# A list-scheduled DeltaNet stage: planner costs from a trace, query decays subtracted on VectorE, first values loaded on their own, output-norm Newton steps on GpSimd

## The chip, the cores and the metric

The kernel runs on one core of a Trainium2 chip. Time is device time in microseconds (us) of one execution. The engines are named as the profile names them: PE is TensorE's matmul row (PEld its weight loads), DVE is VectorE, ACT is ScalarE, POOL is GpSimd, SP is SyncE, whose queue issues most of the DMAs. A row that ends in "q" (SPq, ACTq) is an engine's instruction queue: semaphore waits and DMA issues.

## What is computed

Two layers over 512 latent tokens and 256 context tokens of width 1024, batch 1. Each layer is adaLN-modulated RMSNorm, a mixer, a SiLU gate and a gated residual. Layer 0, which the change is about, is a bidirectional gated DeltaNet with 8 query/key heads and 16 value heads of 128, in chunks of 64 tokens:

```python
p   = u @ w_in                                   # 1024 x 6208
qkv = silu(centred_dwconv(p[..., :4096], conv_w))    # 5 taps; z = the next 2048 columns
beta = sigmoid(ab[:, :, 0]);  g = -exp(a_log) * softplus(ab[:, :, 1] + dt_bias)
gc    = cumsum(g) within a chunk
decay = exp(where(lower, gc[:, None] - gc[None, :], -inf))
a     = where(strict, (k*beta) @ k.T * decay, 0)
t_inv = inverse of (eye + a)                     # unit lower triangular, 64 x 64
qk    = q @ k.T * decay
v_new = t_inv @ (v*beta) - (t_inv @ (k*beta*exp(gc))) @ S
o     = (q*exp(gc)) @ S + qk @ v_new;   S = S*exp(gc_last) + k_dec.T @ v_new
y     = (rms_norm(o) * silu(z)) @ w_out
```

Both directions are run; the state S left by the context is the start for the latents. Layer 1 is grouped-query attention with rotary positions, and the change leaves its code as it is.

## The kernel before

**Stages.** Layer 0 runs in two stages. In the first, up to about 552 us of the profiled execution, everything but the recurrence is made: the adaLN products, the in-projection, the decays, the inverses and q k^T, most of it stored to DRAM buffers (`k_d`, `q_d`, `z_d`, `v_d`, `t_d`, `qk_d`, `gc_d`). In the second, from about 552 to 735 us, the recurrence reads these back, two value heads at a time and 48 steps `x`; the out-projection and layer 1 follow.

**Tiles.** Tokens stand in 6 tiles of 128 (2 of context, 4 of latents). Names carry the tile, `0m` to `5m` for the key side ("m": the matrices to be inverted) and `0q` to `5q` for the query side, and a variant `v` of 0 or 1 for the direction. A decay tile `df` is 128 partitions x 16 heads x 64 columns. f32 products are made of three passes with high and low parts: a weight tile `w` is loaded, ACT writes its high part `wh`, and DVE or POOL writes the rest, `wl = w - wh` (L874).

**The in-projection.** After 8 key heads come 40 heads in the order of a string, "z" and "q" and "v" (L858), each of 24 matmuls of 512 and 24 of 256 columns (`gemm_part`, L885), in one of four PSUM buffers "g". A head's buffers come free when ACT and DVE have run its taps (`acc`, L892 and L900) and its SiLU (`sil_z` L917, `sil_v` L919), so late work on DVE stops PE two or three products later.

**The inverses.** For each tile `t`: a key gram on PE (`G`, L723), masked by DVE and ACT; the decays; products `md`, `mo` of decay and gram on DVE (L672); a transposition on DVE (`L`, L753) and a product with beta on POOL (L758). Two tiles make a pair, and POOL solves three pairs (`X0`, `X1`, `X2`) one after the other: a clearing, then 31 columns of two instructions each (L771, L772), then a weighing with beta (L776; that of `X2` on DVE). Then for each tile the joins: two transpositions `U` on DVE (L790), products `pp` (L799) and `pw` (L823) on PE, and `Tt` on ACT (L811, L830), stored to `t_d`. The query side has its own grams (`GQ`, L840), masks on DVE (`KQ`, L849), decays, and a product on POOL (L672) that is stored to `qk_d` (L855).

**The decays, before.** The rows of `gc` are loaded into `df`, spread over the partitions (`decay_rows`, L686). For m tiles 0 and 1 POOL subtracts a column from all heads in one instruction (`apart`, L705) and ACT makes Abs and Exp of it (`faded`, L710, L711). For the ten other tiles ACT does it alone: one Abs with a bias for each of 16 heads (L698) and one Exp (L700), for both variants.

**What sets the order.** The first stage is written out by a list planner (`written_out`, L1039). Each piece of work has an engine, a cost, a due time, what it comes after, and what buffers it takes and holds (`pool_of`, L1005). The planner gives the next place to the piece that can start first by its own sums (`ready_at`, with a margin for each engine), the one with the lower due time among equals. Costs and due times are thus only numbers in the planner: they set the order of instructions on every engine, and nothing else. Semaphores hold the chip to the dependences, and an instruction that waits holds all that is behind it on its engine.

**Around the recurrence.** The loads for its first step are pieces of the first stage: `first_matrices` (T, QK and the keys) and, after that, `first_values` in two halves (`v_d0`, `v_d1`, L972). DMAs that SP and ACT issue share eight completion semaphores in turn, so that an issue waits for the landing of the DMA eight before it. In steps `x` of 43 to 46 a list `chain` is worked off: the factors of the output norm, for which DVE runs three Newton steps of an inverse root (`rsqrt_steps`, L200 to L202) on 128 x 48 numbers, 3, 3, 3 and then all that is left.

## Time and profile before

| | us |
|---|---|
| time, three runs | 1178.34, 1169.69, 1173.31 (median 1173.31) |
| the profiled execution: its time | 1172.76 |
| its span, first to last instruction | 1171.0 |
| PE busy in it | 1127.3 (96%) |
| DVE, ACT, POOL busy | 784.0, 734.9, 602.6 |
| first stage, PE's first instruction of the recurrence | at 552.01 |
| POOL's solves, first clearing to the end of X2 | 236.19 to about 470.8 |
| mean granted clock of TensorE | 0.989 |

The profile shows one execution. A row of the chain, the waits or the timeline names engine, line, operation and tile; what stands in brackets is idle time of the engine just ahead of that row and what ended it. The granted clock is the share of full clock that TensorE was given.

### The profile page before, as it was taken

To read this page: it belongs to the slowest core of one execution; us is meant where nothing else is said; L and a number is where in the kernel's file an instruction comes from. 1 tells how busy PE (TensorE), PEld (TensorE's weight loads), DVE (VectorE), ACT (ScalarE), POOL (GpSimd) and SP (SyncE) were. 2 spreads that over 40 slices of the span, in tenths; PEclk is the share of its full clock that TensorE was granted. 3 is DMA by queue.
4 is the path that set the end of the run, shared out by engine and by line. 5 is a ranking of instruction groups with operands and counts; after the bars stand their busy time and mean duration, and the time that the engine had idled before them with its cause. 6 is when DMAs were issued, how large, how long until landed. Compare 5 with 4: busy or idle time off the path is not lost. (4 is left out here: it accounts for less than half of the span.)

```text
span 1171.0 us, 27730 instructions
## 1 busy us (share of the span) xinstructions
PE 1127.3 (96%) x10767; PEld 923.8 (79%) x10767; DVE 784.0 (67%) x1645; ACT 734.9 (63%) x1938; POOL 602.6 (51%) x478
## 2 busy tenths in 40 slices
PE   6999999999999799998999999999999999999996
PEld 4777788888888688887666666788887889999885
DVE  5686464899886686873778888345557476667646
ACT  5435544668795966594678998775753246666731
POOL 0252020399999999740475585555744153130810
PEclk9999999999999999999999999899999999999999
DMA  9767745666654834778999993585844112101323
GB/s 366 265 267 265 262 127 176 181 194 177 171 185 153 276 114 150 243 248 248 266 249 251 281 260 96 191 220 183 248 135 135 37 55 73 37 19 55 108 72 90
DMA packets 118901, 208.73 MB, mean 178 GB/s; under 512 B 12497, under 2 KB 77170, under 8 KB 114930
## 3 DMA queue, kind: packets, MB, share of 16 engines
q1 hardware_dynamic: 98834, 195.32, 54.6%
q10 hardware_dynamic: 19936, 11.64, 3.4%
q8 instruction: 85, 1.39, 0.5%
q14 instruction: 46, 0.38, 0.1%
HBM read 166.16 MB, written 40.67 MB: 177 GB/s over the span
## 5 line engine op out<-in xcount | busy, mean ns | idle before, releaser
L1624 PE MATMUL po<-woh,y 128*128 128x512 f32 x384 | 130.3, 404 | 0.3 <-ACT y L1600 0.3
L1466 POOL TENSOR_TENSOR S<-S,glb 128x512 f32<-128x512 f32 x80 | 81.7, 1042 | 75.5 <-PE ks L1457 75.5
L1573 POOL TENSOR_TENSOR wol<-wo,woh 128x1024 fp32r<-128x1024 f32 x32 | 77.1, 2412 | 55.9 <-ACT woh L1566 52.9
L772 POOL TENSOR_TENSOR X<-X,tmp 128x62 f32<-128x62 f32 (+15 forms) x93 | 98.0, 1053 | 7.3
L900 DVE SCALAR_TENSOR_TENSOR acc_v<-g_v,cwv,acc_v 128x510 f32<-128x510 f32 (+3 forms) x128 | 78.2, 614 | 25.1 <-ACT acc_v L892 21.7
L885 PE MATMUL g_z<-uh,wh_z 128*128 128x512 f32 (+1 forms) x256 | 88.0, 344 | 4.7 <-DVE sil_v L919 4.7
L771 POOL TENSOR_TENSOR tmp<-L,X 128x62 f32<-128x62 f32 (+15 forms) x93 | 86.6, 931 | 6.8
L885 PE MATMUL g_v<-uh,wh_v 128*128 128x512 f32 (+1 forms) x256 | 88.1, 344 | 0.0
L885 PE MATMUL g_v<-uh,wl_v 128*128 128x512 f32 (+1 forms) x256 | 86.6, 338 | 0.3 <-issue 0.3
L885 PE MATMUL g_v<-ul,wh_v 128*128 128x512 f32 (+1 forms) x256 | 86.6, 338 | 0.0
L885 PE MATMUL g_z<-uh,wl_z 128*128 128x512 f32 (+1 forms) x256 | 86.1, 336 | 0.0
L885 PE MATMUL g_z<-ul,wh_z 128*128 128x512 f32 (+1 forms) x256 | 86.1, 336 | 0.0
L1624 PEld LDWEIGHTS po<-woh,y 128*128 128x128 f32 x384 | 72.8, 190 | 15.7 <-ACT y L1600 0.7
L1624 PE MATMUL po<-wol,y 128*128 128x512 f32 x192 | 76.1, 396 | 0.3 <-POOL wol L1573 0.3
L1598 DVE SCALAR_TENSOR_TENSOR pt<-pt,og,z 128x128 f32<-128x128 f32 x96 | 34.4, 358 | 34.2 <-PE pt L1589 31.2
L885 PEld LDWEIGHTS g_z<-uh,wh_z 128*128 128x128 f32 x256 | 48.5, 190 | 10.0 <-DVE sil_v L919 5.1
L1531 DVE TENSOR_TENSOR S<-su,S 128x512 f32<-128x512 f32 x80 | 51.6, 687 | 6.0 <-PE su L1517 3.9
L1457 PE MATMUL ks<-S,ck 128*64 128x256 f32 x352 | 55.2, 392 | 0.4 <-ACT o L1463 0.4
L473 DVE SCALAR_TENSOR_TENSOR acc_k<-g_k,cwv,acc_k 128x510 f32<-128x510 f32 (+3 forms) x64 | 39.3, 615 | 22.7 <-ACT acc_k L466 21.0
L885 PEld LDWEIGHTS g_v<-uh,wh_v 128*128 128x128 f32 x256 | 49.2, 192 | 5.7 <-issue 0.4
L885 PEld LDWEIGHTS g_v<-uh,wl_v 128*128 128x128 f32 x256 | 49.1, 192 | 5.2
L885 PEld LDWEIGHTS g_v<-ul,wh_v 128*128 128x128 f32 x256 | 49.1, 192 | 4.8
(440 smaller groups left out, 3336.5 us busy)
## 6 DMA issues: line engine op xcount, KB each, us to landing
aw<-in_ada_late SPq DMA_DIRECT2D x16, 1024.0 KB, 8.5
wo<-in_dn_w_out SPq DMA_DIRECT2D x32, 512.0 KB, 3.9
cv<-v_d SPq DMA_DIRECT2D x48, 256.0 KB, 8.0
aw<-in_ada_first SPq DMA_DIRECT2D x8, 1024.0 KB, 12.3
w_z<-in_dn_w_in SPq DMA_DIRECT2D x16, 512.0 KB, 4.1
w_v<-in_dn_w_in SPq DMA_DIRECT2D x16, 512.0 KB, 4.0
v_d<-vt ACTq DMA_DIRECT2D x16, 384.0 KB, 4.2
cT<-t_d SPq DMA_DIRECT2D x12, 512.0 KB, 8.1
```

What stands on the lines that cost most here:

```text
L473: V.scalar_tensor_tensor(acc[:, c0 + lo:c0 + hi], ps[:, lo + j - 2:hi + j - 2], cwv[:, j, 8 + h:9 + h], acc[:, c0 + lo:c0 + hi], ALU.mult, ...
L771: G.tensor_tensor(tv, bcast(L[:, :, j + 1:, j], 3, j + 1), bcast(X[:, :, j, 0:j + 1], 2, n), ALU.mult)
L772: G.tensor_tensor(X[:, :, j + 1:, 0:j + 1], X[:, :, j + 1:, 0:j + 1], tv, ALU.subtract)
L885: T.matmul(ps[:, :m], w[:, k], u[:, k, c0:c0 + m], start=k == 0 and n_ == 0, stop=k == KT - 1 and n_ == 2)
L900: V.scalar_tensor_tensor(acc[:, c0 + lo:c0 + hi], ps[:, lo + j - 2:hi + j - 2], cwv[:, j, ct:ct + 1], acc[:, c0 + lo:c0 + hi], ALU.mult, A ...
L1457: T.matmul(ks[r0:r0 + 64, w], kq[w][:, hh, r0:r0 + 64], St[hh][:, d], start=True, stop=True)
L1466: G.tensor_tensor(St[hh], St[hh], bcast(g_, 3, P), ALU.mult)
L1531: V.tensor_tensor(St[hh], sj, St[hh], ALU.add)
L1573: G.tensor_tensor(wl, raws.pop(n), halves[n][0], ALU.subtract)
L1598: V.scalar_tensor_tensor(pj, pj, og, raw(z, off, [[st_, 2], [1, 64]]), ALU.mult, ALU.mult)
L1624: T.matmul(acc[:, nh], y[i][:, j, :], ww[k][:, nh * 512:(nh + 1) * 512], start=h == 0 and x == 0, stop=h == VH - 1 and x == 2)
```

## The change

It has four parts.

1. **The list.** Planner costs are replaced by other numbers for many pieces, the due times of grams, joins and query products are changed, the head order is another string, and `wl` of heads 4, 33 and 34 goes from POOL to DVE. The cost of a solve's column stays.
2. **Decays.** `apart` takes an engine from a table. m tiles 0 and 1 stay on POOL; m tiles 2 and 5 and q tiles 0, 1, 2, 4 and 5 are subtracted by DVE, q tile 3 by POOL, each in one instruction for a variant, and ACT then makes one Abs and one Exp of 128 x 1024. m tiles 3 and 4 keep the 16 Abs with bias.
3. **First values.** The first half of `first_values` no longer comes after `first_matrices`, and is due 20 us earlier than the matrices.
4. **Output norm.** For context and the first latents (`gi` 0) the Newton steps are 12 instructions of 128 x 48 on POOL behind two on DVE; the chain is worked off 4, 6, 6 and the rest.

```diff
+    def pool_steps(x, mul):
...
+        steps = [
+            lambda: V.tensor_scalar(x, x, mul, EPS, ALU.mult, ALU.add),
+            lambda: V.tensor_scalar(y.bitcast(I32), x.bitcast(I32), -0.5, float(0x5F3759DF), ALU.mult, ALU.add),
+        ]
+        for i in range(3):
+            to = x if i == 2 else y
+            steps += [
+                lambda: G.tensor_tensor(t, y, y, ALU.mult),
+                lambda: G.tensor_tensor(t, t, x, ALU.mult),
+                lambda: G.tensor_scalar(t, t, -0.5, 1.5, ALU.mult, ALU.add),
+                lambda to=to: G.tensor_tensor(to, t, y, ALU.mult),
+            ]
+        return steps
...
-    def apart(t, v, rows):
+    def apart(t, v, rows, E):
 
         df = dfs[t, v]
-        G.tensor_tensor(df, df, bcast(rows[:, v, t], 2, 64), ALU.subtract)
+        E.tensor_tensor(df, df, bcast(rows[:, v, t], 2, 64), ALU.subtract)
...
-    order = "zqzqzqqzqqzqzqvvzvvzvvzvvzvvzvvzvvvzvzzz"
+    order = "zqzqqqqzzqzqzqvvvzvzvvzvvzvvzvvzvvvzvzzz"
...
-        G_ = n in (1, 2, 3, 4, 33, 34, 35, 36, 37, 38, 39)
+        G_ = n in (1, 2, 3, 35, 36, 37, 38, 39)
...
-                tp_ = Piece("DVE", (3.3, 1.9)[i], e + (0.5, 2.4)[i], taps, n, i, after=[ce], holds=[("g", g[i]), ("acc", a_[0])], lands=0.1)
+                tp_ = Piece("DVE", (3.2, 1.75)[i], e + (0.5, 2.4)[i], taps, n, i, after=[ce], holds=[("g", g[i]), ("acc", a_[0])], lands=0.1)
...
+    APART = (("G", "G", "V", "", "", "V"), ("V", "V", "V", "G", "V", "V"))
+
     def decays(t, r, due, rows):
         out_ = []
         for v in range(2):
             d_ = [r[v]]
-            if t in ((0, 1) if rows is gcM else ()):
-                d_.append(Piece("POOL", 2.5, due + 3 * v - 3, apart, t, v, rows, after=d_, holds=[("df", r[v])], lands=0.1))
+            E = APART[rows is gcV][t]
+            if E:
+                d_.append(Piece({"G": "POOL", "V": "DVE"}[E], {"G": 2.2, "V": 1.25}[E], due + 3 * v - 3, apart, t, v, rows, G if E == "G" else V, after=d_, holds=[("df", r[v])], lands=0.1))
...
-    for t, due in enumerate(T0 + x for x in (26, 0, 100, 136, 140, 175)):
+    for t, due in enumerate(T0 + x for x in (-34, -5, 110, 126, 135, 170)):
...
-        due = T0 + (140, 195, 260, 275, 335, 390)[t]
+        due = T0 + (155, 195, 260, 275, 335, 390)[t]
...
-    for t, due in enumerate(T0 + x for x in (170, 195, 230, 260, 340, 365)):
+    for t, due in enumerate(T0 + x for x in (190, 195, 240, 300, 370, 385)):
...
-    x = T0 + N * SLOT - 60
-    x = Piece("SP", 1.6, x, first_matrices, after=[last["T", 0], last["QK", 0, 0], last["QK", 5, 0], last["QK", 5, 1]], takes=["df", "df", "df"], lands=5.0)
-    x = Piece("SP", 1.2, x.due, first_values, 0, after=[x, last["T", 1]] + [last["v", h] for h in range(8)])
-    Piece("SP", 1.2, x.due + 40, first_values, 1, after=[x] + [last["v", h] for h in range(VH)])
+    at = T0 + N * SLOT - 60
+    Piece("SP", 1.6, at, first_matrices, after=[last["T", 0], last["QK", 0, 0], last["QK", 5, 0], last["QK", 5, 1]], takes=["df", "df", "df"], lands=5.0)
+    x = Piece("SP", 1.2, at - 20, first_values, 0, after=[last["T", 1]] + [last["v", h] for h in range(8)])
+    Piece("SP", 1.2, at + 40, first_values, 1, after=[x] + [last["v", h] for h in range(VH)])
...
+        steps = rsqrt_steps(f, 1.0 / (128.0 * 128.0)) if gi else pool_steps(f, 1.0 / (128.0 * 128.0))
+        return list(times(oss, None, or2)) + steps + list(times(fo, 128.0 ** -0.5, rq))
...
-        if x in (43, 44, 45):
-            some(chain, 3)
-        if x == 46:
-            some(chain, 99)
+        if x in (43, 44, 45, 46):
+            some(chain, (4, 6, 6, 99)[x - 43])
```

Below, instructions stand as they are issued, in the row of one engine; a name ends in the number of its tile, and its trailing digits only tell copies apart.

**PE, where the key gram of tile 1 stands** (`G0_1`, `G1_1`; `g512_q3` is the 512-column product of query head 3). Before:

```order
L885 MATMUL g512_q3_2264<-ul_99,wh_q3_2040 128x512
L885 MATMUL g512_q3_2264<-uh_98,wl_q3_2041 128x512
L723 MATMUL G0_1_2309<-kq0_1m_2248 32x64 x16
L723 MATMUL G1_1_2326<-kq1_1m_2249 32x64 x16
L885 MATMUL g256_q3_2349<-uh_98,wh_q3_2040 128x256
```

After:

```order
L904 MATMUL g256_z3_2503<-ul_99,wh_z3_2192 128x256
L904 MATMUL g256_z3_2503<-uh_98,wl_z3_2193 128x256
L742 MATMUL G0_1_2540<-kq0_1m_2418 32x64 x16
L742 MATMUL G1_1_2557<-kq1_1m_2419 32x64 x16
L956 MATMUL ss_q4_2576<-ones_107,sq_q4_2469 64x1 x12
L904 MATMUL g512_q5_2594<-uh_98,wh_q5_2296 128x512
```

Before, the gram stands in the middle of the 7th of the 40 heads (z0 q0 z1 q1 z2 q2, then q3); after, behind the whole of the 9th (z0 q0 z1 q1 q2 q3 q4 z2 z3): two heads and a half part of 256 columns further on.

**DVE, the first join** (`U_0` reads the solved pair `X0`; `acc_v3` are the taps of value head 3). Before:

```order
L919 SCALAR_TENSOR_TENSOR sil_v1_3640<-g512_v1_3411,acc_v1_3567 128x512
L874 TENSOR_TENSOR wl_v3_3633<-w_v3_3438,wh_v3_3632 128x1024
L790 STREAM_TRANSPOSE U_0_3696<-X0_2640 128x32x32
L919 SCALAR_TENSOR_TENSOR sil_v1_3640<-g256_v1_3542,acc_v1_3567 128x256
L753 STREAM_TRANSPOSE L4_3747<-md_4_3274 128x32x32
L790 STREAM_TRANSPOSE U_0_3696<-X0_2640 128x32x32
```

After:

```order
L724 TENSOR_TENSOR df0_0q_3594<-df0_0q_3594,gcV_92 128x1024
L936 SCALAR_TENSOR_TENSOR sil_z6_3739<-sil_z6_3739,g256_z6_3654 128x256
L724 TENSOR_TENSOR df1_0q_3637<-df1_0q_3637,gcV_92 128x1024
L772 STREAM_TRANSPOSE L4_3788<-md_4_3495 128x32x32
L809 STREAM_TRANSPOSE U_0_3828<-X0_2829 128x32x32
L919 SCALAR_TENSOR_TENSOR acc_v3_3786<-g512_v3_3705,cwv_74,acc_v3_3786 128x510
L919 SCALAR_TENSOR_TENSOR acc_v3_3786<-g512_v3_3705,cwv_74,acc_v3_3786 128x511 x2
```

The join moved from beside value head 1 to ahead of the taps of value head 3, and two new subtractions stand before it.

**POOL, behind the last solve** (`X2`; `wl_z12` is the low part of the weights of gate head 12). Before:

```order
L772 TENSOR_TENSOR X2_4965<-X2_4965,tmp30_2_5893 128x2x31
L672 TENSOR_TENSOR df0_2q_4513<-df0_2q_4513,KQ0_2_4971 128x1024
L672 TENSOR_TENSOR df1_2q_4610<-df1_2q_4610,KQ1_2_4972 128x1024
L874 TENSOR_TENSOR wl_v13_5823<-w_v13_5550,wh_v13_5822 128x1024
L874 TENSOR_TENSOR wl_v14_5926<-w_v14_5691,wh_v14_5925 128x1024
L672 TENSOR_TENSOR df0_3q_4768<-df0_3q_4768,KQ0_3_6043 128x1024
L672 TENSOR_TENSOR df1_3q_4828<-df1_3q_4828,KQ1_3_6044 128x1024
L874 TENSOR_TENSOR wl_z12_6066<-w_z12_5987,wh_z12_6065 128x1024
```

After:

```order
L791 TENSOR_TENSOR X2_4976<-X2_4976,tmp30_2_5866 128x2x31
L691 TENSOR_TENSOR df0_2q_4319<-df0_2q_4319,KQ0_2_4776 128x1024
L691 TENSOR_TENSOR df1_2q_4398<-df1_2q_4398,KQ1_2_4777 128x1024
L724 TENSOR_TENSOR df0_3q_4643<-df0_3q_4643,gcV_92 128x1024
L724 TENSOR_TENSOR df1_3q_4693<-df1_3q_4693,gcV_92 128x1024
L893 TENSOR_TENSOR wl_z12_5817<-w_z12_5620,wh_z12_5816 128x1024
L893 TENSOR_TENSOR wl_v15_5906<-w_v15_5735,wh_v15_5905 128x1024
```

The low parts of v13 and v14 have left POOL, and the two subtractions of q tile 3 stand in their place, ahead of `wl_z12`.

More of the change, by code (lines that the diff above doesn't have):

```diff
@@ L1219, in backbone @@
         ws = [K("SP", 2.7, e - 16 + 3 * kh, late_load, i, nb, kh, takes=["law"], lands=3.0, after=[aws[3, 1], ms_], behind=st_done) for kh in range(2)]
[L1220 removed]
+        pr = [K("PE", 1.88, e - 20, late_product, i, nb, after=ws + through, takes=["gq"], holds=[("law", w) for w in ws], lands=0.1, slack=QUICK)]
         first, through = nb >= 4 or nb < 2, []
@@ L1226, in backbone @@
             for j in range(2 - i):
-                gs = K("PE", 0.6, e - 20, gate_spread, i, nb - 4, j, after=[ra], takes=["gq"], holds=[("lrows", ra)], lands=0.1, slack=QUICK)
+                gs = K("PE", 0.48, e - 20, gate_spread, i, nb - 4, j, after=[ra], takes=["gq"], holds=[("lrows", ra)], lands=0.1, slack=QUICK)
                 through = [gs]
@@ L1231, in backbone @@
         elif not first:
-            tu = K("PE", 1.9, e - 20, late_turned, nb - 2, after=[ra], takes=["gq"], holds=[("lrows", rows_of)], lands=0.1, slack=QUICK)
+            tu = K("PE", 1.72, e - 20, late_turned, nb - 2, after=[ra], takes=["gq"], holds=[("lrows", rows_of)], lands=0.1, slack=QUICK)
             through = [tu]
@@ L1243, in backbone @@
         for i in range(2):
-            g.append(Piece("PE", (5.5, 2.9)[i], t0, gemm_part, n, i, after=[wh, wl] + ([last["g", n - 1]] if n and not i else g), takes=["g"], holds=[("wh", wh)], lands=0.2))
+            g.append(Piece("PE", (5.48, 2.96)[i], t0, gemm_part, n, i, after=[wh, wl] + ([last["g", n - 1]] if n and not i else g), takes=["g"], holds=[("wh", wh)], lands=0.2))
         last["g", n] = g[1]
```

67 lines of the change are left out of this document (34 added, 33 removed).

## The prediction

> **What bounds the kernel now.** I read the engines' shares first, then what PE waits for, then the stages by windows.
>
> ```profile
> PE 1127.3 (96%) x10767; PEld 923.8 (79%) x10767; DVE 784.0 (67%) x1645; ACT 734.9 (63%) x1938; POOL 602.6 (51%) x478
> ```
>
> PE does the same work before and after: no matmul is added or removed. So the change can take away at most what PE idles or runs slowly, and what it can cost is new idling. The span is 1171.0 us, so 43.7 us are idle. The waits of PE, longest first:
>
> ```profile
> PE xt L255 <- DMA ident<-in_ident: 8.1, 1, 8.1
> PE g_z L885 <- DVE sil_v L919: 4.7, 2, 3.6
> PE pr L1483 <- ACT vn L1485: 3.3, 2, 2.7
> PE GQ L840 <- ACT Tt L830: 2.7, 1, 2.7
> PE pa L281 <- DMA aw<-in_ada_first: 2.2, 1, 2.2
> PE pr L1483 <- DVE sil_z L917: 0.9, 1, 0.9
> PE g_q L885 <- DVE wl_q L874: 0.9, 1, 0.9
> ```
>
> (columns: total us, times, longest). The first and the fifth are loads at the start, which stay. The others are what the change can reach: 4.7 + 2.7 + 0.9 + 0.9, or 9.2, up to the recurrence, and 3.3 where it starts. The windows (each stretch's length, then busy time and count of PE, PEld, DVE, ACT, POOL, then the granted clock and the DMAs' share) show slow clock too:
>
> ```profile
> 225.00:250.00 25.00, 24.12 (x238) 21.01 (x237) 24.71 (x34) 19.66 (x53) 16.43 (x18) 1.00 0.48 159
> 275.00:300.00 25.00, 25.00 (x164) 21.97 (x163) 23.58 (x32) 20.12 (x56) 23.75 (x19) 1.00 0.54 167
> 375.00:400.00 25.00, 21.09 (x258) 18.18 (x257) 8.53 (x12) 16.93 (x50) 23.27 (x26) 0.93 1.00 300
> 400.00:425.00 25.00, 22.27 (x127) 19.54 (x128) 24.03 (x33) 22.38 (x57) 23.37 (x24) 1.00 0.54 166
> 554.00:558.00 4.00, 2.58 (x40) 2.26 (x44) 1.75 (x9) 1.70 (x3) 0.00 (x0) 0.57 1.04 292
> 735.00:740.00 5.00, 4.96 (x28) 3.54 (x29) 1.23 (x3) 1.05 (x1) 2.87 (x2) 0.61 0.62 194
> ```
>
> Two things matter. The clock falls (0.93, 0.57, 0.61) only beside a PE stall. And in the first stage PE has two neighbours without slack: DVE (24.71 and 23.58 of 25) and POOL (23.3 to 23.8 of 25 in the rows from 275 to 425). POOL's part is one chain, the three solves:
>
> ```profile
> 236.19 1.81 POOL L764 MEMSET X<- 128x2048 f32 x1
> ...
> 316.71 1.81 POOL L764 MEMSET X<- 128x2048 f32 x1
> 404.26 1.82 POOL L764 MEMSET X<- 128x2048 f32 x1
> ...
> 470.72 5.74 POOL L672 TENSOR_TENSOR df_2q<-df_2q,KQ 128x1024 f32<-128x1024 f32 x2
> ```
>
> 236.19 to 470.72, or 234.5 us for three pairs, the second beginning 80.5 after the first, with no pause in it. In this execution it ends in time: no PE wait names POOL's `wl`. How late it ends in the changed kernel is my main question.
>
> **The decays (part 2).**
>
> ```profile
> L698 ACT ACTIVATE df_2q<-df_2q,gcV 128x64 f32<-128x64 f32 x32 | 8.2, 339 | 13.2 <-DMA df_2q<-gc_d 13.2
> L711 ACT ACTIVATE df_1m<-df_1m 128x1024 f32<-128x1024 f32 x2 | 2.1, 1062 | 0.1
> L705 POOL TENSOR_TENSOR df_1m<-df_1m,gcM 128x1024 f32<-128x1024 f32 x2 | 3.8, 1904 | 0.5 <-DMA df_1m<-gc_d 0.4
> 240.66 1.22 DVE L874 TENSOR_TENSOR wl_z<-w_z,wh_z 128x1024 fp32r<-128x1024 f32 x1
> L874 DVE TENSOR_TENSOR wl_v<-w_v,wh_v 128x1024 fp32r<-128x1024 f32 x13 | 21.4, 1648 | 0.0
> ```
>
> ACT's 32 Abs of a tile cost 8.2 us and become two whole Abs, 2.1: over eight tiles ACT is freed of 8 x 6.1 = 49 us. But ACT is no bound (it is the least busy of the three in most windows), so by itself that is worth nothing beyond the stall behind ACT's wait of 13.2. A subtraction of 128 x 1024 on DVE isn't in the trace; the nearest row, `wl`, of the same form and size, takes 1.22 at its shortest and 1.65 in the mean of 13 beside a busy POOL. Bounds: 14 x 1.22 = 17 to 14 x 1.65 = 23 us more on DVE, plus three `wl` (5). DVE is full in the first windows, but there only the two of tile 2m and one `wl` are new (4 us); the rest falls where it has 3 to 9 us of each 25 free. I put its own time at nothing on PE.
>
> What it costs POOL I read from a pair of rows, the DVE row above and POOL's of the same moment, beside an undisturbed one of the same size:
>
> ```profile
> 240.77 1.51 POOL L772 TENSOR_TENSOR X<-X,tmp 128x174 f32<-128x174 f32 x1
> ...
> 468.50 0.52 POOL L772 TENSOR_TENSOR X<-X,tmp 128x174 f32<-128x174 f32 x1
> ```
>
> A DVE instruction of this form stretches a solve by 1.51 - 0.52 = 1.0 us. Eight of the new ones (5m, 0q, 1q, 2q) fall within the solves: 8 us longer, bounds 0 and 10. [...]
>
> There is a second price. The wait for a `gc_d` load, 13.2 us on ACT, now stands on DVE for 2q, ahead of `wl_z9` and the taps of v6, which free PE's buffers. On ACT it led to these stalls:
>
> ```profile
> 393.94 0.97 PE L840 MATMUL GQ<-kq_2q 128*64 128x64 f32 x16 [2.75 <-ACT Tt L830]
> 402.73 0.49 PE L885 MATMUL g_z<-uh,wh_z 128*128 128x512 f32 x1 [3.56 <-DVE sil_v L919]
> ```
>
> I keep this 6.3 as it is, now at z9 and by way of DVE.
>
> **The list (part 1): when the solves start.** Before, the key gram of tile 1 is issued here:
>
> ```profile
> 206.55 0.39 PE L885 MATMUL g_q<-uh,wh_q 128*128 128x256 f32 x1
> ...
> 209.53 0.40 PE L885 MATMUL g_q<-uh,wh_q 128*128 128x512 f32 x1
> ...
> 215.09 1.10 PE L723 MATMUL G<-kq_1m 128*32 128x64 f32 x64
> ```
>
> A head is thus 3.0 + 5.5 = 8.5 us. After, the gram stands two heads and a 256-column half later, 17.0 + 3.0 and a head's sums (0.8), so at 236. The clearing of `X0` came 21.1 after the gram; half of the subtractions and one of the two products with beta now stand ahead of the last load, so I take 18: **start at 254** (bounds 250 and 257), 18 later than before. Then 234.5 + 8 gives the end of X2 at **497**.
>
> Behind it on POOL stand, in the changed row, two products (5.7), two subtractions of 3q (3.8) and `wl_z12`, 2.4 by this group:
>
> ```profile
> L874 POOL TENSOR_TENSOR wl_z<-w_z,wh_z 128x1024 fp32r<-128x1024 f32 x6 | 14.4, 2398 | 32.3 <-ACT wh_z L871 32.3
> L823 PE MATMUL pw<-pn,U 32*32 32x32 f32 x768 | 7.8, 193 | 0.0
> L790 DVE STREAM_TRANSPOSE U<-X 128x1024 f32<-128x1024 f32 x12 | 25.9, 2173 | 5.7 <-POOL X L776 3.6 <-PE pw L823 2.1
> ```
>
> So `wl_z12` is ready at 497 + 11.9 = 509. Would PE be there? From z12 to the end of the stage it has z12, v15, z13, z14 and z15, 5 x 8.5, and four products of joins (7.8 over six tiles, 1.3 each), query grams and turned heads, together about 8.5 more: 51 us. The stage before ended at 552.0, with 9.2 of stalls and 25 x 0.07 = 1.8 of slow clock in 375 to 400; without them PE would begin z12 at 552 - 11 - 51 = 490. Two stalls ahead of it delay that. One is z9's 6.3. The other is new: `U_0` now stands ahead of v3's taps and waits for `X0`, which is solved and weighed 80.5 and some 4 of stretching after 254, at 338; two transpositions of 2.2, the taps and the SiLU bring v3's first buffer free at about 348. PE has four buffers, v3's two and z7's two, so it can go no further than v4, which stands 11 heads (93.5) and some 11 us of small products behind the gram at 236, at 341: 7 us of stall. So PE comes to z12 at 490 + 6 + 7 = 503 and waits 6 for POOL; the two earlier stalls are covered by this one, since POOL's chain doesn't wait for PE. With a half clock behind it (2) and 1 for v15's weights, next on POOL, the stage ends at 509 + 51 + 3 = **563, against 552: +11**. Bounds: with the start at 250 and no stretching, PE's own 503 decides less one of its stalls, and the stage ends near 550 (-2); with the start at 257, 10 of stretching, and the `qk_d` store of 5q late for its reload, near 572 (+20).
>
> **First values (part 3).**
>
> ```profile
> 554.42 0.33 ACTq L958 DMA_DIRECT2D z_d<-sil_z  x1
> 554.78 0.59 ACT L1485 COPY vn<-pr 128x512 f32<-128x512 f32 x1 [3.29 <-DMA cv<-v_d]
> ...
> SPq L972 <- DMA v_d<-vt: 10.3, 1, 10.3
> 555.42 1.13 PE L1483 MATMUL pr<-cv,cT 64*64 64x128 f32 x16 [2.75 <-ACT vn L1485]
> ```
>
> The last `z_d` store on ACT's queue waits for the landing of `cv`'s second half, whose issue waited 10.3 on SP for the store of v15; `vn`, and PE, wait behind it. With the first half loaded 50 us sooner, the second half takes an earlier place among the eight completions and the store another partner, landed long before. Gone: the 2.75 of PE and what the clock of 0.57 lost in 554 to 562. Half clock over some 6.8 us is 3.4 at most: **-6.1**, bounds -3 and -6.5. Next late would be the `cQK` load behind the store of 5q. [...]
>
> **Newton steps (part 4).**
>
> ```profile
> 727.21 1.27 DVE L200 SCALAR_TENSOR_TENSOR rs<-fo,rs 128x48 f32<-128x48 f32 x1
> ...
> 730.77 0.55 PE L1589 MATMUL pt<-ident,so 128*128 128x128 f32 x3 [1.19 <-ACT o L1463]
> 311.22 0.29 POOL L771 TENSOR_TENSOR tmp<-L,X 128x62 f32<-128x62 f32 x1
> ```
>
> DVE drops about 9 small rows between 716 and 729, ACT's `so` follows `fo`, and PE's stalls of 1.19 and less around 731 bring the slow clock of 735 to 740. POOL's 12 steps are priced from the 128 x 62 row: 12 x 0.3 to 0.4 is 4 to 5 us over three steps `x` of some 3.5 us, so `fo` is there in time. Gain between 0 and 4.5 (all of the stalls and their slow clock); I take **-2.5**.
>
> **Sum**, against the profiled execution (1172.76): +11 - 6.1 - 2.5 = +2.4, and 2 for a late `cQK`: 1177. The profiled time stands 0.6 below the median 1173.31; I leave it at **1177**.
>
> **Rivals.** *The list does what its numbers say* (chance 0.14): if X2 ends by 485, the first stage loses the 9 us of stalls and its slow clock, with -6.1 and -4.5 elsewhere 1153 to 1161. For it: the 13.2 us wait leaves ACT. Against: the gram's place, later by two heads, and the columns' price in the planner, which stays. *DVE becomes the bound, slower* (0.35): the subtractions put loads' waits on DVE, whose late `sil` and taps hold PE's four buffers. A load that is late by over some 6 us costs PE the rest one to one; two such waits of 12, or X0 at 257 with 10 of stretching, give the stage +20 and the kernel 1185 to 1192. For it: DVE's 24.71 of 25 and the 13.2 us. It decides from a stage end of about 568. *Nothing that shows*: ACT's freed 49 us are off the path and the `z_d` store only finds another late partner: 1172 to 1175; it lies within my forecast's own case (0.51, from 1165 to 1185).
>
> **How the numbers follow.** One per cent, 11.7 us, is about what three runs spread over 8.7 us can tell from no change. My case spans 1161.6 to 1185: same 0.51; slower 0.35; faster 0.14. Range 1163 to 1192: +20 - 3 + 2 above; -2 - 6.5 - 2 below, with a little of the faster rival.
>
> **What would show it.** Right: clearing of `X0` near 254, `df_2q` products near 497, PE waiting for POOL's `wl_z12` near 505, no `vn` wait for `cv`, no slow clock near 554. Wrong: X2 ending before 485, or PE waits of over 8 us named for DVE `df` or `sil` before 480, or a new wait for `cQK` larger than the old one.

## The result, and the profile after

The changed kernel takes **1187.4 us** (median of 4 runs, 1185.32 to 1188.19), the kernel before, run beside it, 1173.9 (4 runs, 1169.69 to 1178.34). The ratio is **1.0114, with a 95% interval of 1.0091 to 1.0137**: 13.5 us slower. The forecast was 1177, with a range of 1163 to 1192. The profiled execution of the changed kernel took 1188.19, with a span of 1186.2, against 1171.0 before: 15.2 us longer.

The engines' shares of the changed kernel:

```profile
PE 1132.2 (95%) x10767; PEld 925.0 (78%) x10767; DVE 805.2 (68%) x1653; ACT 691.8 (58%) x1698; POOL 611.6 (52%) x489
```

PE runs the same 10767 matmuls. ACT is 43 us lighter (734.9 before) and DVE 21 us heavier (784.0). PE's waits, longest first:

```profile
PE g_z L904 <- DVE sil_v L938: 9.7, 3, 6.0
PE xt L274 <- DMA ident<-in_ident: 8.0, 1, 8.0
PE pq L1532 <- issue: 3.4, 4, 1.1
PE ht L1769 <- DVE uL L1776: 3.3, 1, 3.3
PE pa L300 <- DMA aw<-in_ada_first: 3.1, 2, 2.3
PE pp L818 <- DVE U L809: 2.1, 1, 2.1
PE su L1540 <- DVE vd L1516: 1.9, 1, 1.9
```

`GQ` waiting for `Tt` (2.7) and `pr` waiting for `vn` (3.3) are gone from the head of the list. In their place stand more waits for DVE, in the first stage (`g_z`, `pp`), at the first steps of the recurrence (`su`) and in layer 1 (`ht`).

**Where the 15.2 us lie.** PE's first product of the recurrence (`pr`) divides the span. It stood at 552.01 and stands at 563.33: **+11.3** in the first stage. From there to the first product of the out-projection it was 181.93 and is 183.34: **+1.4**. What is left, layer 1 above all, went from 437.03 to 439.53: **+2.5**.

The stage's share is read from one window of each kernel, from 200 us to the first `pr` (length, then busy time and count of PE, PEld, DVE, ACT and POOL, the granted clock, the DMAs' share, GB/s). Before:

```profile
200.00:552.01 352.01, 342.42 (x4075) 299.86 (x4073) 261.72 (x369) 255.09 (x630) 269.10 (x225) 1.00 0.63 194
```

After:

```profile
200.00:563.33 363.33, 347.30 (x4075) 302.12 (x4073) 279.14 (x377) 213.89 (x396) 277.34 (x225) 0.97 0.62 188
...
325.00:350.00 25.00, 21.23 (x231) 17.98 (x230) 22.46 (x27) 18.49 (x30) 23.41 (x25) 0.88 0.30 98
400.00:425.00 25.00, 22.38 (x270) 19.43 (x271) 18.09 (x30) 15.43 (x26) 23.27 (x24) 0.89 0.78 252
500.00:525.00 25.00, 21.34 (x239) 17.50 (x239) 21.57 (x29) 19.31 (x30) 19.53 (x8) 0.86 0.89 267
```

The counts are the same, 4075 matmuls. Idle time went from 352.01 - 342.42 = 9.6 to 363.33 - 347.30 = 16.0, **6.4 us more**, and the same matmuls were busy **4.9 us longer**, because the clock fell three times (0.88, 0.89, 0.86). Of the 25 us of each of the three windows DVE has 2.5 or more to spare and ACT 5.7 or more; POOL has 1.6 and 1.7 in the first two, and 5.5 in the last.

The three places, on POOL (the clearings of `X0`, `X1` and `X2`, then what stands behind `X2`):

```profile
253.54 1.82 POOL L783 MEMSET X<- 128x2048 f32 x1
336.41 1.80 POOL L783 MEMSET X<- 128x2048 f32 x1
427.63 1.81 POOL L783 MEMSET X<- 128x2048 f32 x1
493.80 5.72 POOL L691 TENSOR_TENSOR df_2q<-df_2q,KQ 128x1024 f32<-128x1024 f32 x2
499.49 4.74 POOL L724 TENSOR_TENSOR df_3q<-df_3q,gcV 128x1024 f32<-128x1024 f32 x2
504.19 2.37 POOL L893 TENSOR_TENSOR wl_z<-w_z,wh_z 128x1024 fp32r<-128x1024 f32 x1
```

and on PE (in brackets the idle time ahead of the row and what ended it):

```profile
341.27 1.28 PE L818 MATMUL pp<-U,mo 32*32 32x32 f32 x128 [2.08 <-DVE U L809]
343.67 0.50 PE L904 MATMUL g_v<-uh,wh_v 128*128 128x512 f32 x1 [1.12 <-DVE sil_v L938]
345.03 0.79 PE L904 MATMUL g_v<-uh,wl_v 128*128 128x512 f32 x1 [0.56 <-DVE wl_v L893]
...
402.62 0.79 PE L904 MATMUL g_z<-uh,wh_z 128*128 128x512 f32 x1 [6.01 <-DVE sil_v L938]
...
505.07 0.79 PE L904 MATMUL g_z<-uh,wh_z 128*128 128x512 f32 x1 [3.34 <-DVE sil_v L938]
506.62 0.79 PE L904 MATMUL g_z<-uh,wl_z 128*128 128x512 f32 x1 [0.32 <-POOL wl_z L893]
```

The solves start at 253.54 (before 236.19) and end at 493.80 (before 470.72). PE pays at v4 (2.08 + 1.12 + 0.56 = 3.8), at z9 (6.0) and at z12 (3.3 + 0.3). The wait at z9 goes with late loads, of query tile 2's rows on DVE, as this row of DVE shows:

```profile
389.01 2.17 DVE L724 TENSOR_TENSOR df_2q<-df_2q,gcV 128x1024 f32<-128x1024 f32 x1 [5.25 <-DMA df_2q<-gc_d]
```

ACT stood at the same time, 8.92 for a gate head's weights (`w_z`), and finished its part of v6's taps at 394.41, just as DVE came to them; so neither wait sets z9 alone. The loads of both were issued late, from 380.76 on: SP had stood 15.9 us for POOL's product of query tile 0, whose store (`qk_d`) is ahead of them on its queue. The other two places go back to POOL as well. At v4 PE and DVE wait for the weighing of `X0`; ahead of z12 DVE stood 7.14 for the end of `X2`, up to 493.88, before it weighed `X2` and ran the taps and the SiLU that PE waits for.

**The start of the recurrence** in the changed kernel, on SP's queue, on DVE and on PE:

```profile
545.41 2.67 SPq L874 DMA_DIRECT2D qk_d<-df_5q  x2
548.14 0.43 SPq L980 DMA_DIRECT2D cT<-t_d  x1
...
559.24 3.29 SPq L1422 DMA_DIRECT2D elX<-elV  x2
```

```profile
567.63 0.48 DVE L1516 TENSOR_SCALAR vd<-vn,elX 128x128 f32<-128x128 f32 x2 [2.46 <-DMA elX<-elV]
```

```profile
563.33 0.67 PE L1506 MATMUL pr<-cv,cT 64*64 64x128 f32 x16 [0.93 <-DVE sil_z L936]
568.17 0.66 PE L1540 MATMUL su<-vd,ckt 64*64 64x256 f32 x8 [1.92 <-DVE vd L1516]
```

No `vn` waits for `cv` any more, as the prediction had it. But the small load `elX` (state decays with the halves of the partitions exchanged) is issued at 559.24, 4 us behind the row ahead of it on the queue, because its issue waits for landings of the loads before it (3.8 for `cQK` and 2.3 for `ckt`), and `vd` and PE wait for `elX`: 1.92, and half clock from 569.5 on for 6.8 us.

**Layer 1.** One stall is new, with the DVE row that it hangs on:

```profile
912.93 1.13 PE L1769 MATMUL ht<-dn,h 128*128 128x128 f32 x8 [3.34 <-DVE uL L1776]
```

```profile
908.05 2.60 DVE L1973 SCALAR_TENSOR_TENSOR sg<-rope,qg 128x256 f32<-128x256 f32 x1
```

Rows of `sg` around it take 0.41 to 1.26; this one lies beside a subtraction on POOL of 2.54 us. The code there is unchanged, and in a run of the same layer-1 code below (the changed kernel with tile 2's decays on ACT) this stall is absent, while the run with part 2 alone has it too (3.33); how it comes about wasn't followed further. Over the thirteen profiles of this document layer 1 took 435.4 to 439.5 us.

### The profile page after: what moved, and what is told of

Its sections match the earlier page's. It is cut to its first block, busy times and chain, and to the rows that moved or that the text cites. A ratio compares the mean times of both kernels' runs of the same rounds, so it can differ in the third digit from the quotient of the medians.

```text
span 1186.2 us, 27501 instructions
## 1 busy us (share of the span) xinstructions
PE 1132.2 (95%) x10767; PEld 925.0 (78%) x10767; DVE 805.2 (68%) x1653; ACT 691.8 (58%) x1698; POOL 611.6 (52%) x489
## 5 line engine op out<-in xcount | busy, mean ns | idle before, releaser
L790 POOL TENSOR_TENSOR tmp<-L,X 128x62 f32<-128x62 f32 (+15 forms) x93 | 93.3, 1003 | 6.8
L1647 PEld LDWEIGHTS po<-woh,y 128*128 128x128 f32 x384 | 72.3, 188 | 15.9 <-ACT y L1623 0.9
L904 PEld LDWEIGHTS g_z<-uh,wh_z 128*128 128x128 f32 x256 | 49.6, 194 | 15.4 <-DVE sil_v L938 10.2
L464 POOL TENSOR_TENSOR wl_k<-w_k,wh_k 128x1024 fp32r<-128x1024 f32 x8 | 19.1, 2396 | 69.4 <-ACT wh_k L460 62.8
L904 PEld LDWEIGHTS g_z<-uh,wl_z 128*128 128x128 f32 x256 | 49.3, 193 | 6.5 <-POOL wl_z L893 1.0
```

Of the source, the lines that this page charges most:

```text
L790: G.tensor_tensor(tv, bcast(L[:, :, j + 1:, j], 3, j + 1), bcast(X[:, :, j, 0:j + 1], 2, n), ALU.mult)
L904: T.matmul(ps[:, :m], w[:, k], u[:, k, c0:c0 + m], start=k == 0 and n_ == 0, stop=k == KT - 1 and n_ == 2)
L1647: T.matmul(acc[:, nh], y[i][:, j, :], ww[k][:, nh * 512:(nh + 1) * 512], start=h == 0 and x == 0, stop=h == VH - 1 and x == 2)
```

## The experiments

Each ratio is to the kernel before on the same chip, with its 95% interval. "First `pr`" is the end of the first stage, 552.0 before and 563.3 after. A profile is one execution: in five profiles with the order and the decays of before (the kernel before, part 3, part 4, both, and both with `elX` sooner) the first `pr` stands between 550.98 and 553.32, so a difference of 2 us between two profiles can be chance.

### Part 4 alone: Newton steps on POOL

The kernel before, with nothing but the diff's fourth part.

```diff
-        return list(times(oss, None, or2)) + rsqrt_steps(f, 1.0 / (128.0 * 128.0)) + list(times(fo, 128.0 ** -0.5, rq))
+        steps = rsqrt_steps(f, 1.0 / (128.0 * 128.0)) if gi else pool_steps(f, 1.0 / (128.0 * 128.0))
+        return list(times(oss, None, or2)) + steps + list(times(fo, 128.0 ** -0.5, rq))
-        if x in (43, 44, 45):
-            some(chain, 3)
-        if x == 46:
-            some(chain, 99)
+        if x in (43, 44, 45, 46):
+            some(chain, (4, 6, 6, 99)[x - 43])
```

> The kernel before with part 4 alone: the Newton steps of the output norm on GpSimd; the list is the old one. My step priced this at -2.5 us (0 to -4.5): the wait of PE for ACT's o near 731 and the half clock behind it go. Ratio to before about 0.998. If the steps are hidden anyway: 1.000. If GpSimd's twelve steps come late: above 1.000, and PE would wait for fo or so near 731.

1171.92 us, ratio **0.9995 (0.9981 to 1.0008)**: between 2.2 us gained and 0.9 lost, where -2.5 was forecast. The four stalls on PE where the output is turned and projected:

```profile
731.30 0.55 PE L1609 MATMUL pt<-ident,so 128*128 128x128 f32 x3 [0.42 <-ACT o L1483]
732.37 0.67 PE L1503 MATMUL pr<-r,cT 64*64 64x128 f32 x16 [0.52 <-ACT vn L1505]
734.18 0.51 PE L1644 MATMUL po<-woh,y 128*128 128x512 f32 x1 [0.70 <-ACT y L1620]
735.55 0.49 PE L1644 MATMUL po<-wol,y 128*128 128x512 f32 x1 [0.87 <-POOL wol L1593]
```

The same four before were 1.19, 0.53, 0.27 and 0.30. `pt` indeed comes sooner, and then the next two producers, ACT's `y` and POOL's `wol`, are late: 2.3 us of stalls became 2.5. What is gained in this execution is clock alone: half clock over 3.4 us instead of 6.8. The profile of parts 3 and 4 together, with the same steps, has 6.8 again, so that isn't sure either.

### Part 3 alone: first values sooner

The kernel before, with nothing but the third part; only loads on SP's queue move.

```diff
-    x = Piece("SP", 1.2, x.due, first_values, 0, after=[x, last["T", 1]] + [last["v", h] for h in range(8)])
-    Piece("SP", 1.2, x.due + 40, first_values, 1, after=[x] + [last["v", h] for h in range(VH)])
+    x = Piece("SP", 1.2, at - 20, first_values, 0, after=[last["T", 1]] + [last["v", h] for h in range(8)])
+    Piece("SP", 1.2, at + 40, first_values, 1, after=[x] + [last["v", h] for h in range(VH)])
```

> The kernel before with part 3 alone: only SP's queue changes, the first half of cv is loaded earlier. My step priced this at -6.1 us (-3 to -6.5): vn's wait of 3.29 on ACT for the store ahead of it goes, PE's 2.75 with it, and the half clock of 554 to 561. Ratio about 0.995. The rival from the trace of the changed kernel: the next thing late is the load of elX, which takes the wait's place, and at most 1 us is won, ratio 0.999 to 1.000.

1172.61 us, ratio **1.0005 (0.9992 to 1.0018)**: no gain, where -6.1 was forecast. The forecast's mechanism is there: the first half of the values is issued at 423.07 instead of 536.67, and the wait of 2.75 and the half clock behind it are gone. The gain doesn't last. The same two products `pr` of the recurrence, the fifth and the ninth of these rows, in the kernel before (first `pr` at 552.01):

```profile
567.67 0.67 PE L1483 MATMUL pr<-r,cT 64*64 64x128 f32 x16
...
583.43 0.67 PE L1483 MATMUL pr<-r,cT 64*64 64x128 f32 x16
```

and with part 3 (first `pr` at 550.98):

```profile
562.91 0.67 PE L1483 MATMUL pr<-r,cT 64*64 64x128 f32 x16
...
569.81 0.34 PE L1509 MATMUL pq<-vn,cQK 64*64 64x128 f32 x4 [2.15 <-issue]
...
582.12 0.67 PE L1483 MATMUL pr<-r,cT 64*64 64x128 f32 x16
```

From the first `pr`, the fifth stands at 15.7 before and 11.9 here, 3.7 ahead; the ninth at 31.4 and 31.1, 0.3 ahead. Between them lies a stall of 2.15 with 3.4 us of half clock behind it (1.7 lost), together 3.85, about the 3.45 that were lost again. The row names no releaser ("issue"). Some 18 us later both kernels have a stop of this kind without a halving, 0.68 with part 3 and 1.60 before, so that the gain grows again to 1.2 by the end of the recurrence. From 570 to 590, in windows of 5 us, the DMAs' share was 1.03 to 1.12 in both. What holds PE there the profile doesn't name. Nor is the loss the same in each execution: in the profile of parts 3 and 4 together (below), where these steps hold the same instructions, the stops there are 1.15 and 1.07, none halves the clock, and the ninth `pr` is still 1.7 ahead.

### Part 2 alone: the decays, in the order of before

The kernel before, with the table of engines for `apart` and nothing else of the list.

```diff
+    APART = (("G", "G", "V", "", "", "V"), ("V", "V", "V", "G", "V", "V"))
...
-            if t in ((0, 1) if rows is gcM else ()):
+            E = APART[rows is gcV][t]
+            if E:
```

> The kernel before with part 2 alone: the decays by the new table, with the old costs, due times and head order. The gram of tile 1 then stands where it stood (half a head later), so the solves start near 238, not 253.5. If the late start of the solves is what costs the stage its 11 us: X2 ends near 480 (eight stretched pairs, 8 us), the stage within 4 us of before's 552, time 1172 to 1177. If it is the subtractions on VectorE, with their waits for loads and their contention, wherever the solves start: stage near 562, time 1182 to 1188.

1183.68 us, ratio **1.0096 (1.0072 to 1.0119)**. First `pr` at 558.64, 6.6 later than before, mainly from two stalls on PE (the first fence), with POOL's rows for the second:

```profile
402.00 0.80 PE L885 MATMUL g_z<-uh,wh_z 128*128 128x512 f32 x1 [8.15 <-DVE sil_v L919]
486.78 0.50 PE L885 MATMUL g_v<-uh,wl_v 128*128 128x512 f32 x1 [3.00 <-POOL wl_v L874]
```

```profile
479.64 4.75 POOL L705 TENSOR_TENSOR df_3q<-df_3q,gcV 128x1024 f32<-128x1024 f32 x2
484.35 4.73 POOL L874 TENSOR_TENSOR wl_v<-w_v,wh_v 128x1024 fp32r<-128x1024 f32 x2
```

The first stands where the wait on ACT cost 2.75 + 3.56 in two pieces before: it is 8.15 in one, with half clock over 10.2 us (3.4 before). DVE comes late to `sil_v`: it waited 2.06 at the rows of tile 2 and 2.05 for ACT's part of the taps, and ACT had stood 6.51 for the load of `w_z`. As in the changed kernel the store of query tile 0 is ahead of these loads on SP's queue, at 377.88 (before, its second half at 372.82). The second is tile 3's subtraction ahead of the weights of v13. The solves took 239.9 instead of 234.5.

### The list alone

The changed kernel with the old decays; parts 3 and 4 stay in.

```diff
-    APART = (("G", "G", "V", "", "", "V"), ("V", "V", "V", "G", "V", "V"))
+    APART = (("G", "G", "", "", "", ""), ("", "", "", "", "", ""))
```

> The changed kernel with the old decays (one subtraction on GpSimd for tiles 0m and 1m, 16 Abs on ScalarE for the ten others); list, parts 3 and 4 as changed. The grams stand as in the changed kernel, so X0 is cleared near 253; without the subtractions on VectorE the pairs are shorter by up to 8 us (X2's end near 486 to 488 instead of 493.8). If the start governs: 1183 to 1188. If the subtractions on VectorE govern: near 1175.

1184.78 us, ratio **1.0116 (1.0087 to 1.0146)**: no better than the changed kernel. First `pr` at 557.88, 5.9 later than before. So up to the first `pr` the list costs 5.9, the decays 6.6, and both 11.3: they nearly add. But of the 5.9, 2.9 is a wait for the loads of the first step (3.80 in the rows below, where before and in the changed kernel PE waits 0.93 for `sil_z`). The solves took 232.7 here and 240.3 in the changed kernel, so the subtractions stretch them by 7.6 (5.4 in the order of before: 239.9 - 234.5).

Why is the kernel then not 5 us faster than the changed one? The time comes back in the recurrence, which took 189.87 from first `pr` to the first out-product (183.34 in the changed kernel):

```profile
548.19 2.63 SPq L874 DMA_DIRECT2D qk_d<-df_5q  x2
550.86 0.45 SPq L980 DMA_DIRECT2D cT<-t_d  x1
...
557.88 1.13 PE L1506 MATMUL pr<-cv,cT 64*64 64x128 f32 x16 [3.80 <-DMA cT<-t_d]
567.38 1.13 PE L1540 MATMUL su<-vd,ckt 64*64 64x256 f32 x8 [3.83 <-DVE vd L1516]
```

The loads for the first step stand on SP's queue behind the store of the last query tile (`qk_d`, 5q). Here they are issued 7 us ahead of the first `pr`; in the changed kernel 15, before 18 (533.69 to 552.01). PE reaches the end of the stage earlier than its loads, and waits for them: 3.80 and 3.83, with a mean granted clock of 0.66 from 550 to 575.

### Tile 2's decays back on ACT

```diff
-    APART = (("G", "G", "V", "", "", "V"), ("V", "V", "V", "G", "V", "V"))
+    APART = (("G", "G", "V", "", "", "V"), ("V", "V", "", "G", "V", "V"))
```

> The changed kernel with the decays of q tile 2 alone back on ScalarE. DVE then has no wait of 5.25 for that tile's load, ahead of value head 6's taps. My prediction said that the stall at z9 (6.0 us and a half clock behind it) is covered by the one at z12, as GpSimd's chain doesn't wait for PE. By that the wait at z9 shrinks, the one at z12 grows, X2's end stays near 492, and the time stays within 3 us of 1187. If it is not covered: -6 to -9 us, 1178 to 1181.

1180.11 us, ratio **1.0077 (1.0046 to 1.0107)**; the interval overlaps that of the changed kernel. The wait for the load moves to ACT (7.0 us), and PE's stalls at z9 and z12 become:

```profile
404.21 0.79 PE L904 MATMUL g_z<-uh,wh_z 128*128 128x512 f32 x1 [7.07 <-DVE sil_v L938]
...
504.88 0.50 PE L904 MATMUL g_z<-uh,wh_z 128*128 128x512 f32 x1 [0.81 <-DVE sil_v L938]
506.38 0.50 PE L904 MATMUL g_z<-uh,wl_z 128*128 128x512 f32 x1 [0.77 <-POOL wl_z L893]
```

The stall at z9 doesn't go (6.0 in the changed kernel): the loads behind the store of query tile 0 come late (379.84 for the store, SP having stood 18.0 for POOL's product), whichever engine stands waiting for them. X2's products begin at 493.5 and the first `pr` stands at 562.1, only 1.2 sooner. Of the 6.5 us by which this profile is shorter, 1.5 are in the recurrence and 3.7 in layer 1, where it doesn't have the stall of 3.34. So the time fell where it was expected if the stall at z9 is not covered, but not for that reason: the wait at z9 didn't shrink and the one at z12 didn't grow.

### Solves started sooner

The planner's cost of the softplus series (POOL's work ahead of the decays) at 1.0 for 1.25, which moves the solves forward.

```diff
-        v_ = K("POOL", 1.25 * len(ns), g + 14, soft_series, ns, after=[v_], lands=0.1)
+        v_ = K("POOL", 1.0 * len(ns), g + 14, soft_series, ns, after=[v_], lands=0.1)
```

> The changed kernel with one planner cost put back, that of the softplus series on GpSimd (1.25 to 1.0 a term). By that the key heads and the grams stand some 9 us earlier in PE's row, with the decays still on VectorE. If the stage's end follows the start of the solves, X0 is cleared near 245 instead of 253.5, X2 ends near 485 and the stage near 555: about 1179. If the decays on VectorE and their contention are what costs, the start moves and the time stays within 3 us of 1187.

1189.53 us, ratio **1.0140 (1.0120 to 1.0161)**. `X0` is cleared at 246.33, 7.2 sooner, and X2 ends 5.6 sooner, at 488.21; yet the first `pr` comes 2.3 later, at 565.62. Two new waits took the place of the old:

```profile
495.61 0.80 PE L904 MATMUL g_v<-uh,wh_v 128*128 128x512 f32 x1 [5.22 <-DVE sil_v L938]
...
563.76 1.93 PE L842 MATMUL pw<-pn,U 32*32 32x32 f32 x128 [5.78 <-ACT pn L824]
```

In the second, ACT had stood 4.71 behind a store of `Tt`. This run is against my account: I had the end of the stage follow the start of the solves one to one, and it doesn't.

### The small load `elX` sooner

The changed kernel, with the two loads of `elX` as a piece of the list. It was meant for some 60 us ahead of the recurrence; the planner put it at 405.47, 154 us earlier than in the changed kernel (559.24). To make room for `elX` beside the first stage, the scratch tiles of the Newton steps are smaller.

```diff
+    elX = gtile([P, 2, NT, VH], "elX")
...
+    def turned_spans():
+        for hf in range(2):
+            dma(elX[hf * 64:hf * 64 + 64], elV[64 - hf * 64:128 - hf * 64])
+
+    Piece("SP", 0.8, T0 + N * SLOT - 100, turned_spans, after=[elv_], since=T0 + N * SLOT - 100, lands=4.0)
```

> The changed kernel with the two loads of elX (the turned decays of the chunk ends) put into the list some 60 us before its end, in place of the start of the recurrence; only SP's queue changes. If elX's lateness is what ate the gain of part 3, DVE's 2.46 and PE's 1.92 of wait for it near 568 go, and perhaps the half clock of 569 to 576: -2 to -5 us, 1182 to 1185. If another load of the first step is late in its place, no change, 1187.

1181.95 us, ratio **1.0088 (1.0067 to 1.0110)**: 0.67 to 1.10% slower than before, where the changed kernel is 0.91 to 1.37% slower. The two overlap, and how much the load is worth isn't settled. The wait for `elX` is gone, and in its place PE waits for the next loads:

```profile
579.07 0.67 PE L1510 MATMUL pr<-r,cT 64*64 64x128 f32 x16 [1.72 <-DMA cT<-t_d]
587.54 0.45 PE L1536 MATMUL pq<-vn,cQK 64*64 64x128 f32 x8 [2.94 <-issue]
```

From the first `pr` (564.09) to the first out-product it takes 184.84, not less than the 183.34 of the changed kernel. The profiled execution, 1187.14, is the slowest of the four by 5 us, so its rows may not be those of the other three.

### Parts 3 and 4 together, without and with `elX` sooner

The kernel before with both parts (the diffs above), and the same with `elX` moved as in the last run.

> The kernel before with parts 3 and 4, and elX loaded where it was. With elX moved as well the ratio was 0.9966 (0.9952 to 0.9981). If moving elX is what lets the two parts pay: 0.999 to 1.000 here. If the two parts pay together without it: 0.996 to 0.997.

> The kernel before with parts 3 and 4 and elX loaded some 60 us ahead of the recurrence: the old list otherwise, so the stage ends near 551. Each part alone was measured at nothing. If each only uncovers the next late thing, all three together may win what one doesn't: 1166 to 1169, ratio 0.995 to 0.997. If the loads of the first steps, for which the DMA engines are busy without a break, set the pace there, again no difference: 0.999 to 1.001.

1169.23 us, ratio **0.9974 (0.9960 to 0.9988)**, and 1169.15 us, ratio **0.9966 (0.9952 to 0.9981)**. Together the two parts gain 1.4 to 4.7 us in the first run and 2.2 to 5.6 in the second, so `elX` adds nothing that shows. Each alone gained nothing: the product of the two single ratios is 1.0000, with some 0.0019 either way. That the pair is worth more than its parts is at the edge of what these runs resolve. From the first `pr` to the first out-product the pair takes 178.39 in its profile and 180.14 with `elX` sooner, against 181.93 before, 180.35 with part 3 alone and 180.86 with part 4 alone; the two profiles of the pair differ by nearly as much as they gain on the parts.

### A faster version: query products of tile 0 on DVE

On top of the last kernel (parts 3 and 4, `elX` sooner), POOL's products of decay and q k^T for tile 0 go to DVE, and in a second run those of tile 1 too, so that POOL's solves end sooner.

```diff
-            G_ = v == 0 or t not in ()
+            G_ = t != 0
```

> The kernel before with parts 3 and 4 and the early elX, and the two products of q tile 0 on VectorE instead of GpSimd. They then stand ahead of value head 4's SiLU, and the decay tile that q tile 2's load waits for should come free some 10 us sooner. If that buffer, held until GpSimd gets to the product, is why ScalarE stood idle for 11.9 us near 380 and PE near 394 and 403 (2.75 and 3.56, then half clock): ScalarE's idle stretch shrinks below 4 us, both stalls go, -4 to -8 us against the kernel without it, ratio to before 0.990 to 0.994; and the second pair is shorter by the 5 us of the two products. If something else holds that load: no change, 0.996 to 0.998.

> As the kernel with q tile 0's products on VectorE, and q tile 1's as well. GpSimd's second pair is shorter by 10 us in all; X2 ends near 461. If GpSimd's chain still sets anything behind it, another -1 to -3 us; if the stage before is no longer bound by it, no further change, and VectorE's four longer products may cost 1 to 2.

1168.57 us, ratio **0.9964 (0.9946 to 0.9981)**, and 1172.06 us, ratio **0.9990 (0.9974 to 1.0006)**. The first is the lowest time of all, but not to be told from the kernel that it builds on, where 4 to 8 us were expected. ACT's wait for the rows of tile 2 falls from 13 to 5.1 us and the stall at `GQ` goes; the one at z9 stays at 3.8. The loads are issued sooner indeed, at 361.35 for 373.38: in the kernel that it builds on SP stood 15.8 for POOL's product of tile 0, and here 4.6 for DVE's. `X2`'s products begin at 466.6 and, in the second run, at 465.3 (470.1 in the kernel below them), 3.5 and 4.8 sooner where 5 and some 9 were expected. In the second the next wait has grown out of the gain:

```profile
470.42 0.79 PE L905 MATMUL g_v<-uh,wh_v 128*128 128x512 f32 x1 [6.14 <-DVE sil_v L939]
```

DVE, with two tiles' products more, is what PE waits for.

## Why the prediction came out as it did

The time lies 10 us above the forecast and within the range, but outside the case that I gave the best chance (0.51, up to 1185): it fell in the band of the rival with 0.35. The chance for faster than 1% was rightly small; that the slowdown is over 1% is likely but not sure, since its interval (0.91 to 1.37%) reaches across the bound.

**Right: the first stage, +11 forecast, +11.3 in the profile.** The gram of tile 1 was put at 236 and stands at 235.52; `X0` was put at 254 and is cleared at 253.54; X2's end at 497 (493.80); eight subtractions on DVE were to stretch the solves by 8 (7.6 with and without them in the changed order, 5.4 in the old). The upper bound of 10 that I put to this is shown by no run. The eight took 1.21 to 2.87 each in the trace, 15.1 together; the runs show a stretch of half of that or less: 0.5 to 0.8 us for each of ten, since the two of tile 2m, at 254.60 and 256.30, fell within the solves as well.

**The sum of stalls was right, its parts less so.** With no stall and no slow clock I had the stage end at 541, so that 22 us were to be added: 20 of stalls and 2 of slow clock. The trace has 16.0 of stalls, and so about 6 of slow clock. Smaller: v4, 3.8 for 7, since `X0` was weighed some 4 us sooner than I had it, and z12, 3.7 for 7, where the last to come is `sil_v`, late because DVE stood 7.14 for the end of `X2`, and only 0.3 more is POOL's `wl_z12`. Right: z9, 6.0 for 6.3. Mis-sized: "a half clock behind it (2)". I had priced one, at z12; all three stalls brought a stretch of 6.8 us at half clock, 3.4 us where PE is busy through all of it. Stalls put too high and clock put too low cancel, so that the total came out within 0.3 is in part luck.

**Half right: that the two earlier stalls are covered by the one at z12.** With the wait at z9 at 7.1 and that at z12 down from 3.7 to 1.6 (tile 2 on ACT), the stage still ends within 1.2 us of the changed kernel. I also kept z9's 6.3 as a load's lateness, apart from POOL's chain; the load is late because SP stands for POOL's product of query tile 0. But I took the start of the solves for what sets the stage's end, and the run with the solves 7 us sooner ended its stage 2.3 later. By the single runs the list costs 5.9 and the decays 6.6; what PE waits for at the end differs from run to run (a store's landing, a load, POOL's end of `X2`), and no one chain sets the end alone.

**Wrong: "-6.1" for the first values.** The step that failed is the sentence "Gone: the 2.75 of PE and what the clock of 0.57 lost in 554 to 562". Both (in the trace before, the half clock lasts 6.83 us from 554.59) went, in the run with part 3 alone and in the changed kernel, and the time of that run is within 0.9 us gained and 2.1 lost. I asked what would be late next, named the `cQK` load and added 2 for it. Late next was something else: with part 3 alone a stop named "issue" with its half clock, which took 3.45 of the 3.7 us; in the changed kernel the load of `elX`, with its own. The sign to be read was there, a DMA share of 1.04 in a row that I had quoted (554 to 558), and 1.03 to 1.12 in the windows from 570 to 590: PE that came sooner came to the next stop sooner, 2.15 at 569.81. That the loads behind such a share are what holds PE there was not shown.

**Wrong: "-2.5" for the Newton steps**, by its size. The stall of 1.19 shrank to 0.42, and 1.0 us came back at the next two producers on ACT and POOL. Alone, the part gained nothing that can be measured.

**Not foreseen: layer 1, +2.5**, from the stall of 3.34 and its slow clock.

So the 10.8 us between the profiled span and my sum (15.2 for 2.4 + 2) are made up of 0.3 in the first stage, 8.0 in the recurrence (+1.4 for -6.1 - 2.5 + 2 = -6.6) and 2.5 in layer 1.

**The rivals.** *DVE becomes the bound* gave 1185 to 1192, and the time lies there, but the mechanism didn't decide: it asked for a stage end beyond 568, and the stage ended at 563. *The list does what its numbers say* and *nothing that shows* are refuted by the stage: the list alone makes it 5.9 longer.

**What stays open.** Why the list and parts 3 and 4 together (1.0116) are as slow as all four (1.0114) is shown only for the profiled executions, by the loads behind the store of 5q; no run had the loads alone moved ahead of that store. Why parts 3 and 4 gain only together isn't known, nor whether they do. How much `elX` is worth in the changed kernel is open (by the ends of the two intervals, from 2 us lost to 8 gained). The stall in layer 1 was not isolated.

## What to carry to other kernels

A stall that goes at the start of a stage which reloads what the stage before has stored is no gain yet: look at the DMAs' share over the next dozen microseconds, and where it stands at 1 (here 1.03 to 1.12 from 570 to 590), look for the next late arrival before you book anything. In the traces after, follow one and the same instruction some steps further on. And where an order is rebuilt, price each stall with the slow clock behind it (here 6.8 us at half clock with each of three stalls of 3.8, 6.0 and 3.7), and test the parts one by one: here two of four made a kernel that is faster by 0.1 to 0.4%, and the kernel with all four is slower by 1%.

## What the runs showed of the hardware that I had not expected

The price of a stall isn't its length. In the first stage of the changed kernel, stalls of 3.8, 6.0 and 3.7 us were each followed, or overlapped, by 6.8 us at half clock (0.50 from 344.19, 398.80 and 504.61). PE was busy in these stretches for 6.27, 3.00 and 6.04 us, so the clock cost some 3.1, 1.5 and 3.0: the two short stalls lost nearly as much again by the clock as by the wait. The kernel before had a stall of 3.56 with no halving behind it (402.73, with a granted clock of 1.00 from 400 to 425), so not every one of this length brings it. Nor was a long wait in one piece needed: at v4 the longest was 2.08, with 1.3 us of matmuls between it and the next (1.12), and the clock fell at 344.19 all the same. A stall like these three is best priced with 1.5 to 3.1 us more, an estimate from half of PE's busy time in the three stretches.

The clock records of the two kernels, from 150 to 1150 us, have eight stretches at half clock, of 3.41 or 6.83 us:

| kernel | half clock from | for | PE busy in the 3.41 us ahead |
|---|---|---|---|
| before | 394.17 | 3.41 | 0.67 |
| before | 554.59 | 6.83 | 0.67 |
| before | 732.09 | 6.83 | 1.69 |
| changed | 344.19 | 6.83 | 1.79 |
| changed | 398.80 | 6.83 | 1.23 |
| changed | 504.61 | 6.83 | 0.54 |
| changed | 569.47 | 6.83 | 1.49 |
| changed | 914.21 | 3.41 | 1.28 |

The 3.56 of the kernel before lay in two pieces of the same length, 397.58 to 400.99 and 400.99 to 404.41, with 1.59 and 1.68 us of PE busy, and halved nothing, while 1.69 and 1.79 in the table did. So PE's busy time ahead doesn't tell the one from the other, and what decides is not shown. Nor is it the same in each execution: the stall at z9, 3.3 to 4.6 us in the four other profiles with the order and the decays of before, brought 3.4 us of half clock in one and 6.8 in three.

In the first steps of the recurrence PE stops in the middle of a group of matmuls with nothing to wait for that the profile shows ("issue": 1.6 us before, 2.15 with part 3 alone, 2.94 with `elX` sooner). In these traces and that of the changed kernel (1.08) such a stop came to its end 1.3 to 1.6 us after the end of a 16 KB transfer of the kind that the profile calls "instruction" (which took 1.3), while the DMAs' share was above 1.0 (1.06 before, from 585 to 590, and 1.04 in the changed kernel, from 590 to 595). Transfers of this kind without such a stop stand beside them (before, the two that end at 562.51 and 568.92). That the two belong together was not shown.
